# Where the tiles of a two-layer mixer lie in SBUF: a gap at its head, small constants at its end, one query and key buffer fewer

## The chip, the cores and the metric

The kernel runs on one core of a Trainium2 chip. The metric is the device time of one execution in microseconds (us). Operands are 32-bit throughout: the matrix products take them as float32r (4 bytes a column), and each product is made of three matrix multiplications, of high and low halves, to keep float32 accuracy.

## The reference

Two layers of a mixer with three parallel branches over 512 frames of 1024 channels. Cut to what matters:

```
for l in range(2):
    xn = rmsnorm(x, pre_g[l]);  proj = xn @ w_in[l]            # 1024 -> 7584 columns, split into u_a, v_a, z_a, ...
    y_a = u_a * (tril(w_s) @ layernorm(v_a) + b_s) * silu(z_a)       # blocks of 128 frames, 8 groups
    y_b = latent_attention(q_down, kv_down, k_rope) * silu(z_b)      # 8 heads, rotary part shared, chunk mask
    y_c = band_attention(q_c, k_c, v_c, rel_table) * silu(z_c)       # 8 heads, own chunk and 8 before, learned bias
    merged = sum_i sigmoid(g_i + gate_b_i) * (y_i @ w_branch[l, i])  # i over a, b, c; y_i is 512 wide
    x = x + rmsnorm(merged @ w_out[l], post_g[l])
```

## The kernel before

All products go through `mm3` (lines 112 to 115): three matmuls into one PSUM tile, high by high, high by low, low by high. The first operand of a matmul in the listing, `lhsT`, is the stationary one (128 columns, 512 bytes a partition, loaded by a weight load ahead of the matmul); the second, `rhs`, is the moving one, streamed column by column. The profile prints the moving one first: in `pm<-A_h,whi` the tile `A_h` moves and `whi` is stationary. Three kinds of product make up most of the work:

- `fm_unit` (line 197): weights `whi`, `wlo` are stationary, the normalised input `A_h`, `A_l` moves, 512 columns; 24 matmuls a unit.
- `tm_unit` (line 185): slices of `A_h`, `A_l` are stationary and weights move: 512 columns, or 416 in `mla_down`, or 256 twice for the very last unit (line 716).
- the branch products in `gate_units` (line 244 on): weights stationary, and `X` (branches a and c) or `ybh`, `ybl` (branch b) moving, 12 matmuls of 512 columns.

Each weight slice comes by a DMA from SP's queue into `wraw` (3 buffers), ScalarE copies it to `whi`, VectorE or GpSimd makes `wlo` from the rest (line 107; 4 buffers each).

The two attentions are spread over 64 steps a layer (line 655). A step issues the scores of one head and one block of 128 queries (256, 384 or 512 columns; lines 418 to 438), transposes the softmax of three steps earlier (line 361), and after each head makes the weighted sum (lines 378, 379). Between them the list `units` (line 643) is worked off by a credit in microseconds, with fixed rates (line 33): products fill TensorE while the other engines work on the softmax. The order of instructions is fixed when the program is built.

Query and key tiles come from `qtile` (line 142): one head of the latent attention holds four (`qa`, `ka`, `kl`, and the rotary stack `qr`, made by `rope_stack` from line 533), a pair of heads of the band attention six. `qr` of an odd head is made right after the other tiles of its pair.

Where a tile lies in SBUF follows from the listing alone. Pools are laid out one after the other in the order in which they are opened (lines 46 to 49: `cst`, `wp`, `wk`, `sm`), tiles in a pool in the order of their making, and every tile is rounded up to 32 bytes a partition. The first tile starts at byte 16512 of the partition. `ident` (512 bytes) and `mhalf` (32) stand first, so `A_h` starts at byte 17056 = 16 x 1024 + 672; `A_l`, `mrg`, `YT`, `X`, `vt` and `PT_h` follow at 672 past a multiple of 1024 as well, `PT_l` at 160. The constants of the two layers (`col_0`, `gbh_0`, `col_1`, `gbh_1`, 576 bytes) come next, and every tile of `wp` and `wk` then starts at 224 past a multiple of 1024, but `pp1` and `pp2` at 736. Slices that matmuls read start a multiple of 512 bytes into their tile, but the second half of a `mla_down` weight, 1664 bytes into it, and the slices of `X` at line 296, blocks of 256 bytes. So every operand of a float32r matmul starts 32 bytes past a multiple of 64. SBUF is full: the last tile ends 160 bytes before the end of the partition.

Of the kernel before, what the change touches and what calls it, by code (L numbers as in the profile page):

```python
# [8 lines left out]
F32 = mybir.dt.float32  # L9
F32R = mybir.dt.float32r  # L10
# [5 lines left out]
P = 128  # L16
L = 2
D = 1024
S = 512
KT = D // P  # L20
# [3 lines left out]
H = 8  # L24
# [16 lines left out]
def trunk_kernel(ctx, tc, x, wtm, wqd, wrv, wqk, wfm, wgate, wbr, wout,  # L41
                 cols, post_g, ln_g, ln_b, sgu_wt, rel, csnd, out):
    nc = tc.nc
    v_, s_, g_, t_ = nc.vector, nc.scalar, nc.gpsimd, nc.tensor

    cst = ctx.enter_context(tc.tile_pool(name="cst", bufs=1))
    wp = ctx.enter_context(tc.tile_pool(name="wp", bufs=4))
    wk = ctx.enter_context(tc.tile_pool(name="wk", bufs=1))
    sm = ctx.enter_context(tc.tile_pool(name="sm", bufs=4))
    psm = ctx.enter_context(tc.tile_pool(name="psm", bufs=3, space=PSUM))  # L50
    pss = ctx.enter_context(tc.tile_pool(name="pss", bufs=2, space=PSUM))
    pst = ctx.enter_context(tc.tile_pool(name="pst", bufs=2, space=PSUM))
    pso = ctx.enter_context(tc.tile_pool(name="pso", bufs=1, space=PSUM))
    dr = ctx.enter_context(tc.tile_pool(name="dr", bufs=1, space=bass.MemoryType.DRAM))

    ident = cst.tile([P, P], F32, name="ident")
    make_identity(nc, ident)
    mhalf = cst.tile([P, 1], F32, name="mhalf")
    g_.memset(mhalf, -0.5)

    A_h = cst.tile([P, KT, S], F32R, name="A_h")
    A_l = cst.tile([P, KT, S], F32R, name="A_l")
    mrg = cst.tile([P, KT, S], F32, name="mrg")
# [9 lines left out]
    PT_h = cst.tile([P, TB * PTS + P], F32R, name="PT_h")  # L73
    PT_l = cst.tile([P, TB * PTS + P], F32R, name="PT_l")
    x1 = dr.tile([S, D], F32, name="x1")


    ZB = 3 * PTS + 2 * P
# [61 lines left out]
        return mrg[:, 2 * tb:2 * tb + 2, :]  # L140

    def qtile(nm):
        return wk.tile([P, S], F32R, name=nm, tag="qk", bufs=12)

    def bk_t(n):
        return wk.tile([P, n], F32, name="bk", tag="bk", bufs=2)
# [28 lines left out]
        return i  # L175

    def load_consts(l):
        t = cst.tile([P, 4 * KT + H + 3], F32, name=f"col_{l}")
        nc.sync.dma_start(out=t, in_=cols[l])
        c = {"pre": t[:, 0:KT], "gb": t[:, KT:4 * KT], "sb": t[:, 4 * KT:4 * KT + H], "mg": t[:, 4 * KT + H:]}  # L180
        c["gbh"] = cst.tile([P, 3 * KT], F32, name=f"gbh_{l}")
        g_.tensor_scalar(out=c["gbh"], in0=c["gb"], scalar1=0.5, scalar2=None, op0=ALU.mult)
        return c

# [141 lines left out]
    def ca_qk(l, kind, p, qk):  # L326

        a, b = qtile("qa"), qtile("qb")
        kl = (qtile("kl"), qtile("kl")) if kind else None
        qk[(kind, p)] = (a, b, kl)  # L330
        lo, hi = slice(0, 64), slice(64, 128)

        def done(ps):
            if kind == 0:
                for t, r, o in ((a, lo, hi), (b, hi, lo)):
                    s_.activation(out=t[r], in_=ps[r], func=AF.Copy, scale=0.125)
                    v_.scalar_tensor_tensor(out=t[o], in0=ps[r], scalar=0.125, in1=f32(t[r]),
                                            op0=ALU.mult, op1=ALU.subtract)
            else:
                for t, u, r, o in ((a, kl[0], lo, hi), (b, kl[1], hi, lo)):  # L340
                    s_.copy(out=t[r], in_=ps[r])
                    v_.tensor_tensor(out=u[r], in0=ps[r], in1=f32(t[r]), op=ALU.subtract)
                    s_.copy(out=t[o], in_=ps[r])
                    g_.tensor_copy(out=u[o], in_=u[r])
        yield from fm_unit(wfm[l, kind * 4 + p], done)
# [187 lines left out]
    def rope_stack(h, d):  # L533

        r = qtile("qr")
        hh, j = divmod(h, 4)
        rs = slice(j * 32, j * 32 + 32)
        v_.tensor_copy(out=r[0:32], in_=YT[rs, 2 * hh, :])
        s_.copy(out=r[32:64], in_=YT[rs, 2 * hh + 1, :])
        g_.tensor_copy(out=r[64:128], in_=r[0:64])  # L540
        d[h] = r
# [44 lines left out]
    for tb in range(TB):  # L586
        for hf in range(2):
            nc.sync.dma_start(out=x_rows(tb)[:, hf, :], in_=x[tb * P:(tb + 1) * P, hf * 512:(hf + 1) * 512])
        if tb == 0:
            cl = [load_consts(0)]  # L590
            raws += [load_raw(wqd[0, j], 832) for j in range(2)]
        if tb == 1:
            raws.append(load_raw(wqd[0, 2], 832))
# [4 lines left out]
    for l in range(L):  # L598
        c = cl[l]
        qk, zc, zb, st = {}, {}, {}, {}  # L600
        ya, yc, yb = [], [], []
        if l == 0:
            dgen = mla_down(l, st, raws, first)
            del raws
            step(dgen)
            norm_x(2, c)
            norm_x(3, c)
            cl.append(load_consts(1))
        else:
            st = st1  # L610
# [44 lines left out]
        for i in range(NS + LAG + 1):  # L655
# [32 lines left out]
            while credit > 0 and units and units[0][0] <= i:  # L688
                t = next(units[0][1], None)
# [14 lines left out]
        for hf in range(2):  # L704
            t = bk_t(S)
# [117 lines left out]
```

## Time and profile before

| what | us |
|---|---|
| median of 3 runs (lowest, highest) | 1101.63 (1100.35, 1102.0) |
| the profiled execution's own time | 1102.16 |
| its span, first to last instruction | 1100.4 |
| TensorE busy in the span | 1075.0 |
| VectorE, ScalarE, GpSimd busy | 645.7, 529.2, 234.1 |

Times of the trace are counted from the start of the span. A matmul's printed duration (about 0.39 us for 512 columns) runs from the entry of its first column to the modelled end of its last result, and overlaps that of the next; the pace of TensorE is the distance from one matmul's start to the next one's. The views used here are the profile's page, the waits, the groups by line and shape, the windows (busy time by stretch) and the timeline (single instructions in order of time).

### The profile page before, as it was taken

What the parts mean: (1) busy time and instruction counts of PE and PEld (TensorE: products, weight loads), DVE (VectorE), ACT (ScalarE), POOL (GpSimd) and SP (SyncE); (2) the same over time, 40 slices, a digit from 0 to 9 for tenths busy, and PEclk for the clock granted to TensorE, in tenths of its full rate; (3) what the DMA queues carried; (4) which work ended last, traced back from release to release, by engine and by line L of the source; (5) the groups of instructions that cost most, each with busy time, mean ns of one, the idle gap of its engine ahead of it and who ended that gap; (6) DMA issues with size and microseconds to landing.
All of it is one profiled execution on the core that took longest, in us unless ns stands there. A gap on an engine that the chain in (4) does not pass through costs nothing.

```text
span 1100.4 us, 14199 instructions
## 1 busy us (share of the span) xinstructions
PE 1075.0 (98%) x5096; PEld 886.9 (81%) x5096; DVE 645.7 (59%) x1332; ACT 529.2 (48%) x1073; POOL 234.1 (21%) x249
## 2 busy tenths in 40 slices
PE   6999999999999999999999999999999999999997
PEld 4887878888888888888787787788888888888886
DVE  5674776666566654334577756675656665534443
ACT  6454576445454543224563644664544545432331
POOL 2310132221123231210033111331212323221000
PEclk9999999999999999999999999999999999999999
DMA  7231132223233223334342322212223232323342
GB/s 238 78 101 63 52 102 85 70 81 101 77 96 96 69 86 109 95 114 153 104 133 92 104 74 67 85 58 87 91 73 106 89 86 79 102 77 96 106 150 80
DMA packets 37703, 104.65 MB, mean 95 GB/s; under 512 B 5376, under 2 KB 6400, under 8 KB 37632
## 3 DMA queue, kind: packets, MB, share of 16 engines
q1 hardware_dynamic: 37632, 103.74, 30.3%
q8 instruction: 40, 0.66, 0.3%
q14 instruction: 31, 0.25, 0.1%
HBM read 99.53 MB, written 4.19 MB: 94 GB/s over the span
## 4 chain that ended last, share of the span: by engine, by line
PE 45%; ACT 2%; DVE 2%; issue 1%; POOL 1%; DMA 0%; POOLq 0%; DVEq 0%; ACTq 0%
PE pm L114 13%; PE pm L113 13%; PE pm L115 13%; PE pt L361 2%; PE po L379 1%; PE po L378 1%; DVE wlo L107 0%; PE ps_s L419 0%; PE ps_s L418 0%; PE ps_s L436 0%; PE ps_s L438 0%; PE ps_s L437 0%; POOL rs L136 0%; PE pt L167 0%; DMA wraw<-in_wtm_dram 0%
## 5 line engine op out<-in xcount | busy, mean ns | idle before, releaser
L102 ACT CAST whi<-wraw 128x1024 fp32r<-128x1024 f32 (+3 forms) x194 | 177.1, 914 | 263.2 <-PE pm L114 156.9
L113 PE MATMUL pm<-A_h,whi 128*128 128x512 f32 x640 | 259.9, 406 | 0.0
L114 PE MATMUL pm<-A_l,whi 128*128 128x512 f32 x640 | 252.8, 395 | 0.0
L115 PE MATMUL pm<-A_h,wlo 128*128 128x512 f32 x640 | 252.7, 395 | 0.0
L107 DVE TENSOR_TENSOR wlo<-wraw,whi 128x1024 fp32r<-128x1024 f32 (+3 forms) x130 | 152.0, 1172 | 113.2 <-ACT whi L102 109.7
L107 POOL TENSOR_TENSOR wlo<-wraw,whi 128x1024 fp32r<-128x1024 f32 (+1 forms) x64 | 116.2, 1815 | 379.7 <-ACT whi L102 311.7
L113 PE MATMUL pm<-whi,A_h 128*128 128x512 f32 (+2 forms) x456 | 177.9, 390 | 2.6 <-ACT A_h L172 2.6
L114 PE MATMUL pm<-wlo,A_h 128*128 128x512 f32 (+2 forms) x456 | 176.1, 387 | 1.1 <-DVE wlo L107 1.1
L115 PE MATMUL pm<-whi,A_l 128*128 128x512 f32 (+2 forms) x456 | 176.3, 387 | 0.4 <-DVE A_l L173 0.2
L115 PEld LDWEIGHTS pm<-A_h,wlo 128*128 128x128 f32 x640 | 120.1, 188 | 29.1
L114 PEld LDWEIGHTS pm<-A_l,whi 128*128 128x128 f32 x640 | 120.4, 188 | 25.2
L113 PEld LDWEIGHTS pm<-A_h,whi 128*128 128x128 f32 x640 | 120.2, 188 | 25.2
L113 PEld LDWEIGHTS pm<-whi,A_h 128*128 128x128 f32 x456 | 86.5, 190 | 20.2 <-ACT A_h L172 4.5
L115 PEld LDWEIGHTS pm<-whi,A_l 128*128 128x128 f32 x456 | 86.4, 189 | 17.4 <-DVE A_l L173 2.0
L114 PEld LDWEIGHTS pm<-wlo,A_h 128*128 128x128 f32 x456 | 86.5, 190 | 17.0 <-DVE wlo L107 2.2
L354 DVE TENSOR_SCALAR pp<-pp,st 128x128 f32<-128x128 f32 (+3 forms) x128 | 70.2, 549 | 3.6
L367 ACT CAST PT_h<-pt 128x128 fp32r<-128x128 f32 (+3 forms) x128 | 53.9, 423 | 32.1 <-PE pt L361 31.0
L423 DVE CUSTOM_DVE_ANT_0 pp<-ps_s,bk 128x128 f32<-128x128 f32 (+1 forms) x64 | 31.2, 487 | 60.4 <-PE ps_s L419 60.1
L368 DVE TENSOR_TENSOR PT_l<-pt,PT_h 128x128 fp32r<-128x128 f32 (+3 forms) x128 | 61.6, 481 | 6.5 <-ACT PT_h L367 6.1
L361 PE MATMUL pt<-ident,pp 128*128 128x128 f32 x320 | 55.9, 272 | 1.5 <-DVE X L212 1.5
L444 ACT ACTIVATE pp<-ps_s,st 128x128 f32<-128x128 f32 (+1 forms) x64 | 33.8, 528 | 43.4 <-DVE st L442 42.7
L426 ACT ACTIVATE pp<-pp,st 128x128 f32<-128x128 f32 (+1 forms) x64 | 36.0, 563 | 37.6 <-DVE st L425 36.9
(180 smaller groups left out, 1581.8 us busy)
## 6 DMA issues: line engine op xcount, KB each, us to landing
wraw<-in_wgate_dram SPq DMA_DIRECT2D x48, 512.0 KB, 3.6
wraw<-in_wtm_dram SPq DMA_DIRECT2D x32, 512.0 KB, 3.5
wraw<-in_wfm_dram SPq DMA_DIRECT2D x32, 512.0 KB, 3.6
wraw<-in_wbr_dram SPq DMA_DIRECT2D x48, 256.0 KB, 2.6
wraw<-in_wout_dram SPq DMA_DIRECT2D x16, 512.0 KB, 3.6
bk<-in_rel_dram SPq DMA_DIRECT2D x16, 256.0 KB, 2.7
wraw<-in_wqd_dram SPq DMA_DIRECT2D x8, 416.0 KB, 4.2
mrg<-in_x_dram SPq DMA_DIRECT2D x8, 256.0 KB, 6.9
```

The source lines that it names most:

```text
L102: s_.copy(out=hi[:, :cols], in_=raw[:, :cols])
L107: i = e.tensor_tensor(out=lo[:, :cols], in0=raw[:, :cols], in1=f32(hi[:, :cols]), op=ALU.subtract)
L113: t_.matmul(out=ps, lhsT=lh, rhs=rh, start=start, stop=False)
L114: t_.matmul(out=ps, lhsT=lh, rhs=rl, start=False, stop=False)
L115: t_.matmul(out=ps, lhsT=ll, rhs=rh, start=False, stop=stop)
L354: v_.tensor_scalar(out=pp[:, :n], in0=pp[:, :n], scalar1=rc, scalar2=None, op0=ALU.mult)
L361: t_.transpose(pt[:, kb * P:(kb + 1) * P], pp[:, kb * P:(kb + 1) * P], ident)
L367: s_.copy(out=dst(PT_h), in_=src)
L368: v_.tensor_tensor(out=dst(PT_l), in0=src, in1=f32(dst(PT_h)), op=ALU.subtract)
L423: v_.tensor_tensor_reduce(out=pp[:, :n], in0=ps[:, :n], in1=bias[:, S - n:S], scale=1.0, scalar=-3e38, op0=ALU.add, op1=ALU.max, accum_out=mx)
L426: s_.activation(out=pp[:, :n], in_=pp[:, :n], func=AF.Exp, bias=nm, accum_out=se)
L444: s_.activation(out=pp[:, :n], in_=ps[:, :n], func=AF.Exp, bias=nm, accum_out=se)
```

## The change

A tile `pad` of 480 float32 (1920 bytes) is placed first in `cst` and never used. `ident`, `mhalf` and the constants of the layers move to a new pool `cs` that is opened after `sm`. To make room, the query and key tiles have 11 buffers instead of 12. No instruction is added, taken out or changed, besides the places of its operands and what follows from the buffers.

By the rules above `A_h` then starts at 16512 + 1920 = 18432 = 18 x 1024; `A_l`, `mrg`, `YT`, `X`, `vt`, `PT_h` at multiples of 2048, `PT_l` at 512 past a multiple of 1024, `wraw`, `whi`, `wlo` and all of `wk` at multiples of 1024 (`pp1`, `pp2` 512 past one). Every operand of a float32r matmul but the two exceptions named starts at a multiple of 512, those at multiples of 128 and 256. `ident`, which moves in the transposes, stays at 128 past a multiple of 512.

```diff
+    cs = ctx.enter_context(tc.tile_pool(name="cs", bufs=1))
...
-    ident = cst.tile([P, P], F32, name="ident")
-    make_identity(nc, ident)
-    mhalf = cst.tile([P, 1], F32, name="mhalf")
-    g_.memset(mhalf, -0.5)
-
+
+    cst.tile([P, 480], F32, name="pad")
     A_h = cst.tile([P, KT, S], F32R, name="A_h")
...
     x1 = dr.tile([S, D], F32, name="x1")
+    ident = cs.tile([P, P], F32, name="ident")
+    make_identity(nc, ident)
+    mhalf = cs.tile([P, 1], F32, name="mhalf")
+    g_.memset(mhalf, -0.5)
...
     def qtile(nm):
-        return wk.tile([P, S], F32R, name=nm, tag="qk", bufs=12)
+        return wk.tile([P, S], F32R, name=nm, tag="qk", bufs=11)
...
-        t = cst.tile([P, 4 * KT + H + 3], F32, name=f"col_{l}")
+        t = cs.tile([P, 4 * KT + H + 3], F32, name=f"col_{l}")
...
-        c["gbh"] = cst.tile([P, 3 * KT], F32, name=f"gbh_{l}")
+        c["gbh"] = cs.tile([P, 3 * KT], F32, name=f"gbh_{l}")
```

## Rows read from the trace of the kernel before

**Rows 1.** The page: busy us (share) xinstructions, and TensorE's granted clock in 40 slices.
```profile
PE 1075.0 (98%) x5096; PEld 886.9 (81%) x5096; DVE 645.7 (59%) x1332; ACT 529.2 (48%) x1073; POOL 234.1 (21%) x249
PEclk9999999999999999999999999999999999999999
```

**Rows 2.** Waits of TensorE: us in total, times, longest us.
```profile
PE pt L167 <- DVE tmp L164: 10.2, 5, 7.1
PE pm L113 <- ACT A_h L172: 2.6, 2, 2.4
PE pt L361 <- DVE X L212: 1.5, 2, 0.8
```

**Rows 3.** Windows, columns as headed: attention in both layers, then gates alone.
```profile
core 0: us, PE busy (x) PEld busy (x) DVE busy (x) ACT busy (x) POOL busy (x), PEclk, DMA share, GB/s
150.00:250.00 100.00, 100.00 (x488) 83.44 (x487) 63.79 (x144) 55.02 (x116) 28.73 (x22) 1.00 0.28 85
1000.00:1050.00 50.00, 50.00 (x216) 40.06 (x215) 24.89 (x27) 17.88 (x25) 6.24 (x5) 1.00 0.41 120
```

**Rows 4.** Timeline of TensorE (start us, us, ...): gates of branch c, layer 2.
```profile
999.79 0.39 PE L113 MATMUL pm<-A_h,whi 128*128 128x512 f32 x1
...
1004.69 0.39 PE L113 MATMUL pm<-X,whi 128*128 128x512 f32 x1
```

**Rows 5.** The same view: output product of layer 1, then the end of layer 2's.
```profile
509.89 0.40 PE L113 MATMUL pm<-whi,A_h 128*128 128x512 f32 x1
...
514.79 0.40 PE L113 MATMUL pm<-whi,A_h 128*128 128x512 f32 x1
...
1084.68 0.39 PE L114 MATMUL pm<-wlo,A_h 128*128 128x512 f32 x1
...
1088.34 0.39 PE L115 MATMUL pm<-whi,A_l 128*128 128x512 f32 x1
```

**Rows 6.** The same view: a product of branch b.
```profile
411.17 0.39 PE L115 MATMUL pm<-ybh,wlo 128*128 128x512 f32 x1
...
412.53 0.39 PE L115 MATMUL pm<-ybh,wlo 128*128 128x512 f32 x1
```

**Rows 7.** The same view: the last unit, 256 columns a matmul.
```profile
1088.57 0.28 PE L113 MATMUL pm<-whi,A_h 128*128 128x256 f32 x1
...
1093.90 0.28 PE L115 MATMUL pm<-whi,A_l 128*128 128x256 f32 x1
```

**Rows 8.** The same view: scores of one block of queries, and the product after them.
```profile
102.85 0.28 PE L436 MATMUL ps_s<-ka,qa 128*128 128x256 f32 x1
...
103.21 0.39 PE L113 MATMUL pm<-whi,A_h 128*128 128x512 f32 x1
```

**Rows 9.** Groups of TensorE by line and shape: xcount | busy us, mean ns | idle before.
```profile
L113 PE MATMUL pm<-A_h,whi 128*128 128x512 f32 x640 | 259.9, 406 | 0.0
L113 PE MATMUL pm<-whi,A_h 128*128 128x512 f32 x376 | 149.2, 397 | 0.0
L361 PE MATMUL pt<-ident,pp 128*128 128x128 f32 x320 | 55.9, 272 | 1.5 <-DVE X L212 1.5
L113 PE MATMUL pm<-X,whi 128*128 128x512 f32 x128 | 51.2, 400 | 0.0
L113 PE MATMUL pm<-whi,A_h 128*128 128x416 f32 x64 | 24.3, 382 | 2.6 <-ACT A_h L172 2.6
L520 PE MATMUL pt<-ident,YT 128*32 128x128 f32 x8 | 1.5, 271 | 0.0
```

**Rows 10.** Timeline: rotary stack of head 3 on VectorE; last scores of head 1.
```profile
120.08 0.42 DVE L538 CAST qr<-YT 32x512 fp32r<-32x512 f32 x1
...
131.45 0.39 PE L438 MATMUL ps_s<-krs,qr 128*128 128x512 f32 x1
150.01 0.28 PE L438 MATMUL ps_s<-krs,qr 128*128 128x256 f32 x1
```

## The prediction

> **What bounds the kernel now.** I read the page first: TensorE is busy 98% of the span, and its granted clock is full in every slice, so the level is 2.4 GHz throughout [rows 1]. The waits come next: of the 25 us in which TensorE is idle, the largest wait is 10.2 us for `norm_x` at the joins of the stages, and inside the attention only single waits below a microsecond are left [rows 2]. The windows tell the same from the other side: in 100 us of attention TensorE is never idle while VectorE is busy 64%, and in the gate stage it is never idle at VectorE's 50% [rows 3]. No other engine and no transfer sets the pace over most of the span. The time is therefore the number of matmuls times the distance from one start to the next, and the question is what that distance depends on. Only the timeline shows it.
>
> At 2.4 GHz 512 columns enter in 213.3 ns and 256 in 106.7. The timeline shows more, and not the same everywhere:
> - Weights stationary, `A_h`/`A_l` or `X` moving: 4.90 us over 21 distances, 233.3 ns [rows 4].
> - `A` stationary, weights moving: 233.3 ns as well in the first half of the output product, yet 3.66 us over 16, 228.8 ns, in the second half [rows 5].
> - `ybh`/`ybl` moving: 1.36 us over 6, 226.7 ns [rows 6].
> - 256 columns, weights moving: 5.33 us over 47, 113.4 ns [rows 7]; 256 columns in the scores: 0.36 us over 3, 120 ns [rows 8].
>
> The first class is the same with the other engines at work and nearly idle, so they don't cause it. What differs is where the operands lie: `A` and `X` begin 672 past a multiple of 1024, weights, `yb` and the query tiles 224 past one. So the place in SBUF bears on the pace, by about 2% between classes, and all classes are 6 to 12% above bare entry.
>
> **How I read the distances.** Sixteen columns of 4 bytes, 64 bytes a partition, enter in 6.67 ns at 2.4 GHz. 113.4 ns is 17.0 of these, 226.7 is 34.0, 233.3 is 35.0, 120 is 18.0; 228.8 is 34.3, a mean. Bare entry would be 16 and 32. Every operand now starts 32 bytes past a multiple of 64 (the layout in the section on the kernel). If the moving operand is fetched in 64-byte pieces that start at multiples of 64, then 2048 bytes touch 33 pieces instead of 32 and 1024 bytes touch 17 instead of 16. No settled distance above is below 33 or 17, and the 256-column stream sits on 17 exactly. That is an estimate from five distances; no matmul of the trace with aligned operands at full rate contradicts or confirms it, since there is none (the transposes move an aligned `ident`, but at half this rate).
>
> **The change, part by part.** *The gap and the moved constants.* After it every moving and stationary operand starts at a multiple of 64, nearly all at multiples of 512. By the reading above each matmul loses one piece, 6.67 ns. How many are there? 5096 matmuls on the page [rows 1], less 464 transposes (six lines, the first and the last of them with x320 and x8 [rows 9]), makes 4632: 1920 with `A` moving (three lines of x640), 384 with `X`, 1128 with weights moving at 512 columns, 192 at 416 [rows 9], and the rest in branch b, the scores and the weighted sums.
> - 4632 x 6.67 ns = 30.9 us.
> - `sgu_mix` moves four blocks of 64 columns, so it loses four pieces each: 48 x 3 further pieces, 1.0 us more.
> - The `mla_down` matmuls of layer 1 are paced by loads and norms, as the waits on L167 and L113 [rows 2] show: 96 x 6.67 ns = 0.6 us not gained.
> - What is late next: a TensorE that is 3% faster reaches its waits earlier. The joins stay as long as they are. In attention VectorE at 64% [rows 3] has to do the same in 3% less time, which leaves it at 66%. Between nothing and one wait of 0.75 us (1.5 us, 2 times [rows 2]) for each of 32 heads, 24 us, I take 2 us, near the first end, since softmax is consumed three steps after it is made.
>
> Sum: 30.9 + 1.0 - 0.6 - 2.0 = 29.3 us less. The profiled execution took 1102.16 us (span 1100.4 and 1.8 around it), 0.5 above the median of the runs; 1102.2 - 29.3 = 1072.9, or 1072 on the median's footing.
>
> The bounds of the piece: I can't show that it vanishes. From below, the addresses might change nothing, or the distances might rise to the 120 ns that the scores take, one piece more [rows 8]. From above, everything beyond 33 and 16 pieces might go. One piece is the middle of these and what rows 7 have in excess.
>
> *Constants at the end.* `ident` keeps its place within 512 bytes and moves at half rate; `mhalf`, `col` and `gbh` are operands of single columns. Nothing on either side, hidden by a full TensorE [rows 3]. [...]
>
> *Eleven query and key buffers.* Twelve tiles are alive when `qr` of an odd head is made while the odd head of the pair before is still in use: `qr` of head 3 is cast at 120.08, head 1's last scores, which free four tiles, start at 131.45, and head 3 needs it at 150.01 [rows 10]. With eleven it has to be made after 131.7, still 18 us early. I count nothing, as a wait in that window meets a tile nobody yet needs. The far end: if the cast kept its place in VectorE's queue it would hold the splits and softmax behind it by 11.4 us, in three odd heads and one tile of the last pair in each layer, 8 x 11.4 = 91 us. I hold that for unlikely, as a buffer is only handed out behind its release and the cast can then be queued behind it.
>
> [...] The rows show that two places, both multiples of 32, differ by 2% [rows 4, 6]. If pieces are of 16 or 32 bytes, all operands already lie well, no piece is gained, and the classes differ for another reason; this is the third rival below. [...]
>
> [...]
>
> **The rivals.**
> 1. *All excess beyond one piece goes* (33 pieces at 512 columns, the classes become one): `A` and `X` moving and the slow 224 of the weights-moving matmuls lose 13.3 ns (2304 + 224: 33.7 us), 904 others 8.8 (8.0 us), the remaining 432 of 512 columns some 10 (4.3 us), 768 shorter ones one piece (5.1 us): 51 us less, 1051. For it: the classes' differences look like costs of place as well. Against it: rows 6 with 34.
> 2. *Only the relation of the two operands counts.* In rows 6 both lie at the same place modulo 512 and 34 pieces are the result; after the change all do. Then 2528 matmuls go from 35 to 34, and 904 from 34.3 to 34: 16.9 + 1.9 us less, 1083. Against it: the scores also have both at the same place and take 18, not 17.
> 3. *Address is not the cause*, or what it does is the same at 0 as at 32: 1102, within 0.2%.
> 4. *Slower: two reads that start at the same place collide.* Place: every product with `A`, where the operands now lie 64 bytes apart modulo 512. Price: rows 8 against rows 7, one piece: (1920 + 384 + 1128 + 192 + 48) x 6.67 ns = 24.5 us, 1126. It decides if rows like 4 come out above 233.3 ns. For it: 120 against 113.4 ns at 256 columns. Against it: rows 6, same place and the fastest of all with 512.
>
> **How the numbers follow.** One piece per matmul 0.45, with its own range 1057 (the 2304 of rows 4 lose a second piece, 15.4 us) to 1087 (half a piece in the mean). Rival 1: 0.17. Rival 2: 0.12. Rival 3: 0.11. Rival 4: 0.15, which takes in a loss through the buffers. 0.2% of the time, 2.2 us, is about what a measurement here can tell from none. Faster by more than that: 0.45 + 0.17 + 0.12 = 0.74; within it 0.11; slower 0.15. The range leaves out rival 4 and the low tail of rival 1: 1045 to 1103.
>
> **What would show it.** Right: rows 4's distance at 226.7 ns or less, rows 7's at 106.7 to 109, the stage of gates alone shorter by 3% with TensorE's clock unchanged, no new wait above a few us, `qr` of head 3 cast after 131 and before its head. Wrong: distances as now (rival 3), `A` moving at 226.7 with rows 7 unchanged (rival 2), distances above 233.3 or 113.4 (rival 4), or VectorE's casts at L538 waiting on TensorE with idle TensorE behind them (the buffers).

## The result and the profile after

The changed kernel takes 1084.65 us (median of 4 runs, 1083.68 to 1085.38) against 1101.0 us (1100.35 to 1102.0) before: ratio 0.985, interval 0.9833 to 0.9867. Its profiled execution took 1085.38 us with a span of 1083.7, so 16.7 us of span are gone. The forecast of 1072 us had the direction, and the time lies in its range; the likeliest case was not what happened. 1084.65 us is close to the 1083 us of the second rival, which had a chance of 0.12.

First the page of the changed kernel, to be read against [rows 1]: busy us (share), instructions, and the granted clock.

```profile
PE 1058.5 (98%) x5096; PEld 886.0 (82%) x5096; DVE 648.1 (60%) x1332; ACT 529.1 (49%) x1073; POOL 231.3 (21%) x249
PEclk9999999999999999999999999999999999999999
```

TensorE executes the same 5096 matmuls at the same granted clock (0.999 of full in the mean, 0.997 before), and is busy 16.5 us less. So it isn't waits that went. The waits of TensorE (us in total, times, longest us) say the same; all are those of [rows 2], two lines further down in the listing, within 0.2 us, and TensorE is idle 25.2 us of the span against 25.4:

```profile
PE pt L169 <- DVE tmp L166: 10.1, 5, 7.0
PE pm L115 <- ACT A_h L174: 2.8, 2, 2.6
PE pt L363 <- DVE X L214: 1.5, 2, 0.8
```

The windows answer to [rows 3], with the same columns: attention, then the gates alone (the second window begins 15 us earlier than before, as the stage does).

```profile
150.00:250.00 100.00, 100.00 (x495) 84.63 (x495) 65.71 (x147) 55.57 (x118) 27.81 (x23) 1.00 0.27 85
985.00:1035.00 50.00, 50.00 (x222) 41.38 (x222) 26.28 (x29) 18.76 (x26) 6.32 (x5) 1.00 0.42 129
```

TensorE is never idle in either, as before. In the same time it starts 222 matmuls of the gates instead of 216 and 495 of attention instead of 488, 2.8% and 1.4% more. VectorE rises to 66% in attention and still sets nothing.

The timeline of TensorE in the changed kernel (start us, us, ...) has the distances, in the order: scores of one block; transposes and what follows them, with a product of branch b; output product of layer 1; gates of layer 2; output product of layer 2 and the last unit.

```profile
103.30 0.28 PE L438 MATMUL ps_s<-ka,qa 128*128 128x256 f32 x1
...
103.66 0.40 PE L115 MATMUL pm<-whi,A_h 128*128 128x512 f32 x1
...
403.17 0.60 PE L363 MATMUL pt<-ident,pp 128*128 128x128 f32 x4
403.53 0.48 PE L115 MATMUL pm<-A_h,whi 128*128 128x512 f32 x1
403.84 0.40 PE L116 MATMUL pm<-A_l,whi 128*128 128x512 f32 x1
404.07 0.39 PE L117 MATMUL pm<-A_h,wlo 128*128 128x512 f32 x1
...
406.34 0.39 PE L115 MATMUL pm<-ybh,whi 128*128 128x512 f32 x1
...
407.48 0.39 PE L117 MATMUL pm<-ybh,wlo 128*128 128x512 f32 x1
...
503.14 0.39 PE L115 MATMUL pm<-whi,A_h 128*128 128x512 f32 x1
...
507.90 0.39 PE L115 MATMUL pm<-whi,A_h 128*128 128x512 f32 x1
...
984.83 0.39 PE L115 MATMUL pm<-A_h,whi 128*128 128x512 f32 x1
...
989.59 0.39 PE L115 MATMUL pm<-X,whi 128*128 128x512 f32 x1
...
1066.08 0.39 PE L115 MATMUL pm<-whi,A_h 128*128 128x512 f32 x1
...
1071.52 0.28 PE L115 MATMUL pm<-whi,A_h 128*128 128x256 f32 x1
...
1075.12 0.28 PE L115 MATMUL pm<-whi,A_h 128*128 128x256 f32 x1
```

What the reader is to see, distance by distance:
- `A` or `X` moving: 4.76 us over 21 distances, 226.7 ns, where [rows 4] have 233.3.
- Weights moving over `A`: 226.7 ns in layer 1 (503.14 to 507.90, 21 distances) and at the end of layer 2 (1066.08 to 1071.52, 24 distances in 5.44 us), where [rows 5] have 233.3 and 228.8.
- `yb`: 1.14 us over 5, 228 ns with rounding at both ends, against the 226.7 of [rows 6]: nothing gained.
- The last unit, 256 columns: 3.60 us over 30, **120.0 ns**, where [rows 7] have 113.4: longer. The scores stay at 120 ns (0.36 us over 3), as in [rows 8].
- Behind transposes the first distances are 0.31 and then 0.23 us, and it takes several matmuls until 226.7 is reached: averaged over the 84 places where `A` moves behind a group of transposes, the second distance is 231.5 ns, the fifth 228.1 and the eleventh 226.8.

Every class of 512 columns now settles at the distance of the fastest class before, and none settles below it. I took the mean distance of each class on both timelines, without the distances next to a transpose and those with a wait in them: `A` moving 233.36 to 227.81 ns (1828 distances, 10.2 us), `X` moving 233.28 to 227.18 (376, 2.3 us), weights moving at 512 columns 230.25 to 227.59 (1112, 3.0 us), `yb`, scores and weighted sums of 512 columns together 1.0 us, the last unit 0.3 us to the other side. That is 16.2 us of the 16.7 that the span lost; the scores and weighted sums of 256 and 384 columns give some 0.5 us more.

### The profile page after: what moved, and what is told of

Read it like the earlier page. It is cut to its first block, busy times and chain, and to the rows that moved or that the text cites. A ratio compares the mean times of both kernels' runs of the same rounds, so it can differ in the third digit from the quotient of the medians.

```text
span 1083.7 us, 14197 instructions
## 1 busy us (share of the span) xinstructions
PE 1058.5 (98%) x5096; PEld 886.0 (82%) x5096; DVE 648.1 (60%) x1332; ACT 529.1 (49%) x1073; POOL 231.3 (21%) x249
## 4 chain that ended last, share of the span: by engine, by line
PE 43%; ACT 3%; DVE 2%; issue 1%; DMA 1%; POOL 1%; POOLq 0%; DVEq 0%; ACTq 0%
PE pm L116 12%; PE pm L115 12%; PE pm L117 12%; PE pt L363 2%; PE po L381 1%; PE po L380 1%; ACT whi L104 0%; PE ps_s L421 0%; PE ps_s L420 0%; PE ps_s L438 0%; DMA wraw<-in_sgu_wt_dram 0%; PE ps_s L440 0%; DVE wlo L109 0%; PE ps_s L439 0%; ACT tmp L162 0%
## 5 line engine op out<-in xcount | busy, mean ns | idle before, releaser
L104 ACT CAST whi<-wraw 128x1024 fp32r<-128x1024 f32 (+3 forms) x194 | 177.4, 916 | 247.0 <-PE pm L116 146.7
L115 PE MATMUL pm<-A_h,whi 128*128 128x512 f32 x640 | 257.0, 402 | 0.0
L117 PE MATMUL pm<-A_h,wlo 128*128 128x512 f32 x640 | 249.8, 390 | 0.0
L116 PE MATMUL pm<-A_l,whi 128*128 128x512 f32 x640 | 249.5, 390 | 0.0
L115 PE MATMUL pm<-whi,A_h 128*128 128x512 f32 (+2 forms) x456 | 176.7, 388 | 2.8 <-ACT A_h L174 2.8
```

The source lines that it names most:

```text
L104: s_.copy(out=hi[:, :cols], in_=raw[:, :cols])
L115: t_.matmul(out=ps, lhsT=lh, rhs=rh, start=start, stop=False)
L116: t_.matmul(out=ps, lhsT=lh, rhs=rl, start=False, stop=False)
L117: t_.matmul(out=ps, lhsT=ll, rhs=rh, start=False, stop=stop)
```

## The experiments

**Which address counts? Two kernels that set the two readings against each other.** The first is the kernel before with 32 bytes ahead of everything: each operand starts at a multiple of 64, and all stay where they were relative to each other.

```diff
     cst = ctx.enter_context(tc.tile_pool(name="cst", bufs=1))
...
+    cst.tile([P, 8], F32, name="pad")
     ident = cst.tile([P, P], F32, name="ident")
```

> The kernel before with 32 bytes of gap at the head and nothing else: A, X at 704 and weights, yb, query tiles at 256 past a multiple of 1024, all operands at multiples of 64, their distance from one another as before (64 bytes modulo 512). Theory 'relation' (the pace depends on where moving and stationary operand start relative to one another): rows with A moving stay at 233.3 ns, time 1101 us within 0.3%. Theory 'piece' (each operand's own start modulo 64 counts): at least what the whole change gave, 1085 us or less, A moving at 227 ns or less.

Measured: 1100.66 us, ratio 0.9996 (0.9987 to 1.0006). The gates of layer 2 on its timeline:

```profile
1004.35 0.39 PE L114 MATMUL pm<-X,whi 128*128 128x512 f32 x1
...
1005.05 0.39 PE L114 MATMUL pm<-X,whi 128*128 128x512 f32 x1
```

Three distances in 0.70 us: still 233.3 ns, and over the whole timeline `A` moving has a mean of 233.35 ns, as before the change. The second is the other way round, the kernel after with its gap 32 bytes longer: every operand starts 32 past a multiple of 64, as before the change, and all keep one place relative to each other.

```diff
-    cst.tile([P, 480], F32, name="pad")
+    cst.tile([P, 488], F32, name="pad")
```

> The changed kernel with a gap 32 bytes longer: every operand 32 bytes past a multiple of 512, all still at the same place modulo 512. 'Relation': as the changed kernel, 1084.6 us within 0.3%, A moving at 226.7 ns. 'Piece': the gain goes, 1100 us or so, A moving at 233 ns.

Measured: 1084.03 us, ratio to before 0.9849 (0.9832 to 0.9865). The same stage:

```profile
1003.97 0.39 PE L115 MATMUL pm<-A_h,whi 128*128 128x512 f32 x1
...
1004.65 0.39 PE L115 MATMUL pm<-X,whi 128*128 128x512 f32 x1
```

0.68 us over three, 226.7 ns; the mean of `A` moving is 227.7 ns, against 227.8 after the change. Multiples of 64 without a common place give nothing; a common place without multiples of 64 gives all of it. The theory of the lost piece falls by both.

**Which part of the change?** The kernel after without the gap and with twelve buffers, so that only the constants are moved; the operands then start 128 past a multiple of 1024.

```diff
-    cst.tile([P, 480], F32, name="pad")
...
-        return wk.tile([P, S], F32R, name=nm, tag="qk", bufs=11)
+        return wk.tile([P, S], F32R, name=nm, tag="qk", bufs=12)
```

> Only the constants move behind the other pools; no gap, 12 buffers: operands at 128 past a multiple of 1024, all at the same place modulo 512. 'Relation' and 'piece' both: as the changed kernel, 1084.6 us within 0.3%, so that neither the gap nor the multiples of 1 KB nor the eleventh buffer matter. If multiples of 1 KB matter by themselves: between 1085 and 1101 us.

Measured: 1085.96 us, ratio 0.9869 (0.9854 to 0.9883), an interval that overlaps that of the whole change. Gates of layer 2:

```profile
984.78 0.39 PE L114 MATMUL pm<-A_h,whi 128*128 128x512 f32 x1
...
989.54 0.39 PE L114 MATMUL pm<-A_h,whi 128*128 128x512 f32 x1
```

4.76 us over 21, 226.7 ns: moving the small tiles away from between `A` and `X` and the rest is what counts, since it was the 576 bytes of the layers' constants that set the two groups apart (672 against 224 past a multiple of 1024). The gap and the loss of a buffer are not needed for that. All four runs (1085.86 us and more) lie above the four of the whole change (up to 1085.38); no run here tells what these 1.3 us between the medians are.

The buffers alone, in the kernel before:

```diff
-        return wk.tile([P, S], F32R, name=nm, tag="qk", bufs=12)
+        return wk.tile([P, S], F32R, name=nm, tag="qk", bufs=11)
```

> The kernel before with 11 query and key buffers and nothing else. If the buffer costs nothing, as I counted: 1101 us within 0.3%, and the cast of head 3's rotary stack after 131 us. If a wait on the freed buffer holds VectorE: slower, by up to 91 us, with TensorE idle in the attention.

Measured: 1100.65 us, ratio 1.0005 (0.9996 to 1.0014). On its timeline the rotary stack of head 3 is made 12 us later than in [rows 10], with a wait of 1.67 us on VectorE:

```profile
132.29 0.42 DVE L538 CAST qr<-YT 32x512 fp32r<-32x512 f32 x1 [1.67 <-PE ps_s L436]
```

and the waits of TensorE have nothing new; the longest is still that of `norm_x`:

```profile
PE pt L167 <- DVE tmp L164: 9.5, 5, 6.6
```

**Every place by itself.** This kernel leaves the mixer out and runs streams of 40 matmuls: the moving tile lies at a multiple of 512 bytes, the stationary one at 0, 32, ... 480 past one (`wa` to `wp`), with 512 columns, with 256, and with 512 in reverse order.

```diff
+    mv = cst.tile([P, 4, S], F32R, name="mv")
+    for i in range(16):
+        ws.append((cst.tile([P, S + 8], F32R, name="w" + "abcdefghijklmnop"[i]), 0))
...
+            t_.matmul(out=ps[:, :n], lhsT=w[:, e + (k % 4) * P:e + (k % 4 + 1) * P], rhs=mv[:, k % 4, :n],
+                      start=k == 0, stop=k == count - 1)
```

> A kernel that leaves the mixer out: it only runs streams of 40 matmuls, one moving tile at a multiple of 512, and nineteen stationary tiles that start 0, 32, 64, ... 480 bytes (wa to wp) and 4, 8 and 16 bytes (wq, wr, ws) past it; 512 columns, then 256, then 512 in reverse order. 'Relation': the settled distance depends on the stationary tile's place: wa 226.7 ns, wc (64 bytes, as A moving before the change) 233.3, wo (448, as weights moving before) 228.8 or 233.3; at 256 columns wa 120 and wo 113.3 ns. If another cause lies behind the classes (the three products' pattern, the other engines, PSUM), all nineteen give one distance. Unknown to every theory: whether a place is faster than wa; if one settles at 33 pieces, 220 ns, a layout with it would beat the changed kernel.

Its timeline (each row a stream; the next start less this start, over 40, is the mean distance). The letters shown: `wa` lies at 0, `wc` at 64, `wd` at 96, `wi` at 256, `wj` at 288, `wo` at 448.

```profile
24.98 9.50 PE L70 MATMUL pm<-mv,wc 128*128 128x512 f32 x40
34.32 9.52 PE L70 MATMUL pm<-mv,wd 128*128 128x512 f32 x40
...
80.80 9.24 PE L70 MATMUL pm<-mv,wi 128*128 128x512 f32 x40
89.88 9.49 PE L70 MATMUL pm<-mv,wj 128*128 128x512 f32 x40
...
136.52 9.33 PE L70 MATMUL pm<-mv,wo 128*128 128x512 f32 x40
...
182.87 4.96 PE L70 MATMUL pm<-mv,wa 128*128 128x256 f32 x40
...
192.40 4.72 PE L70 MATMUL pm<-mv,wc 128*128 128x256 f32 x40
196.96 4.96 PE L70 MATMUL pm<-mv,wd 128*128 128x256 f32 x40
...
309.81 9.50 PE L70 MATMUL pm<-mv,wo 128*128 128x512 f32 x40
```

No other engine works beside these streams, and at 512 columns they have the distances of the kernels. Settled means of the last 24 distances, by the place of the stationary operand less that of the moving one, against the kernels:

| place | streams, ns | kernels, ns |
|---|---|---|
| 0 | 226.7 | 226.7, `yb` before [rows 6] and all after |
| 64 | 233.3 | 233.3, `A` moving before [rows 4] |
| 192 and 448 | 228.9, and 448 once 233.3 | 228.8 and 233.3, weights moving before [rows 5] |
| 256 | 226.7 | |
| the others, steps of 32 | 232.1 to 234.4 | |
| 0, 256 columns | 120.0 | 120, scores [rows 8] and last unit after |
| 64 and 320, 256 columns | 113.3 and 117.8 | |
| 192 and 448, 256 columns | 117.8 | 113.4, last unit before [rows 7] |

So at 512 columns the relation repeats after 256 bytes, not after 512 as the rival had it, and at 256 columns the common place is among the slowest. The same place (448) settles at either of two distances, in rows of 9.33 us in one pass and 9.50 in the other, as the two halves of [rows 5] did. The last line of the table seems to differ, but the kernel with 11 buffers, whose operands of the last unit lie 448 from each other as in the kernel before, has the streams' number there: 5.53 us over 47, 117.7 ns.

```profile
1086.76 0.28 PE L113 MATMUL pm<-whi,A_h 128*128 128x256 f32 x1
...
1092.29 0.28 PE L115 MATMUL pm<-whi,A_l 128*128 128x256 f32 x1
```

In that kernel the second half of layer 2's output product, just ahead of it, stayed at 233.3 ns instead of going to 228.8. So this place has two settled distances at 256 columns too, and the 113.4 of [rows 7] is one of them.

**The relation moved on purpose.** Two kernels from the one after, with a tile between `A`, `X` and the rest: 256 bytes, which by the streams changes nothing, and 96, which by them should take all of the gain away, though every operand still starts at a multiple of 32.

```diff
+    cst.tile([P, 64], F32, name="pad2")
     x1 = dr.tile([S, D], F32, name="x1")
```

> The changed kernel with 256 bytes more between the first pool and the weights: A, X at multiples of 512, weights, yb and query tiles 256 past one. The streams by themselves gave 226.7 ns at 0 and at 256 alike. 'Relation modulo 256': as the changed kernel, 1084.6 us within 0.3%. If the whole 512 bytes (or equal places as such) mattered: near 1101.

Measured: 1083.89 us, ratio 0.9848 (0.9831 to 0.9864). Gates of layer 2, 18 distances in 4.08 us, 226.7 ns:

```profile
984.98 0.39 PE L116 MATMUL pm<-A_h,whi 128*128 128x512 f32 x1
...
989.06 0.39 PE L116 MATMUL pm<-X,whi 128*128 128x512 f32 x1
```

```diff
+    cst.tile([P, 24], F32, name="pad2")
     x1 = dr.tile([S, D], F32, name="x1")
```

> The same with 96 bytes: weights, yb and query tiles 96 past a multiple of 512, A and X at 0. From the streams: A or X moving at 234.3 ns (wd), weights moving at 233.3 (wf), yb at 226.7. 'Relation': slower than the kernel before, which has 229 ns in four fifths of the weights-moving matmuls: 2304 x 1 ns + 904 x 4 ns = 6 us, less 1 us in the attention, some 1106 us (ratio 1.004 to 1.006). 'Piece' (all operands are at multiples of 32): 1101 or less.

Measured: 1104.13 us, ratio 1.0034 (1.0021 to 1.0047): slower than before, though by a little less than the 1.004 to 1.006 expected. Output product of layer 1, 21 distances in 4.90 us, 233.3 ns; the mean of `A` moving is 234.0, near the 234.3 of the stream at 96:

```profile
508.20 0.39 PE L116 MATMUL pm<-whi,A_h 128*128 128x512 f32 x1
...
513.10 0.40 PE L116 MATMUL pm<-whi,A_h 128*128 128x512 f32 x1
```

Between two groups of tiles, 96 bytes instead of 256 cost 20.2 us here (1104.13 less 1083.89).

**Whose relation, and what of the load?** More streams without the mixer: the place changes with each matmul, so that either a matmul's own two operands agree (`own`) or it agrees with the weights loaded for the next one (`nxt`); the stationary tile has 64 or 32 columns instead of 128; and the place goes in steps of 4 bytes from 0 to 252.

```diff
+        mm(own, (wa, wb)[k % 2], 0, P, (mva, mvb)[k % 2], S, k, 48)
...
+        mm(nxt, (wb, wa)[k % 2], 0, P, (mva, mvb)[k % 2], S, k, 48)
...
+            stream(w, 0, mcols, mva, S, 48)
...
+        ps = stream(wa, e, P, mva, S, 36)
```

> Streams alone again, the mixer left out. First 40 as wa before: 226.7 ns. Then two streams in which moving and stationary tile both alternate between 0 and 64 past a multiple of 512: 'own', where each matmul's two operands agree and the stationary one loaded meanwhile for the next lies 64 off, and 'next', where the one loaded meanwhile agrees with the moving one and its own lies 64 off. If moving read and the weight load that runs beside it disturb each other: next 226.7 ns and own 229 to 234. If a matmul's own pair counts: the other way. Then stationary tiles of 64 and of 32 columns at 0 and 64: if the disturbance is the load's reading, the excess over 213.3 ns falls with the columns loaded; if the moving read alone makes it, it stays at 13 and 20 ns. Then the stationary tile at 0, 4, 8, ... 252 bytes: a map in steps of 4 bytes; a place under 226.7 ns would be one to build a layout on.

The rows of the narrow stationary tiles, at place 0 and 64 each (48 distances to the next start):

```profile
38.55 11.19 PE L65 MATMUL pm<-mva,wa 128*64 128x512 f32 x48
49.58 11.33 PE L65 MATMUL pm<-mva,wb 128*64 128x512 f32 x48
60.75 11.28 PE L65 MATMUL pm<-mva,wa 128*32 128x512 f32 x48
71.86 11.29 PE L65 MATMUL pm<-mva,wb 128*32 128x512 f32 x48
```

Settled, `own` and `nxt` both have 231.7 ns: neither pair alone gives 226.7, and that part decides nothing. With 64 columns loaded the two places have 230.0 and 232.7 ns, with 32 both have 231.7, where 128 columns gave 226.7 and 233.3: the difference of place shrinks with the load and is gone at 32, yet the pace doesn't come down to 226.7. Over the 213.3 ns that 512 columns take at 0.417 ns a column (bare entry, an estimate from 226.7 ns at 512 columns and 120.0 at 256 in the streams before and after these) that is an excess of 17 to 19 ns, so neither of the two outcomes expected came: it doesn't fall with the columns loaded, and it doesn't stay at 13 and 20. In steps of 4 bytes 226.7 is reached at 0, 120, 132, 144, 156, 204 and 252, most places lie between 230 and 235, the highest at 237.7 (164 bytes), and none settles below 226.7.

**Which data, which length?** The same streams with bfloat16, and with 448 down to 128 columns.

```diff
+    mh = cst.tile([P, 4, S], BF, name="mh")
+    wh = cst.tile([P, S + 256], BF, name="wh")
...
+    for n in (448, 384, 320, 256, 192, 128):
+        stream(wa, 0, mva, n, 40)
+        stream(wb, 0, mva, n, 40)
```

> Streams alone, the mixer left out: float32r 512 columns at the same place, then bfloat16 operands, 512 columns, the stationary tile 0, 32, 64, 128 and 192 bytes past the moving one's place, then float32r with 448, 384, 320, 256, 192 and 128 columns, each at 0 and at 64 bytes. If the disturbance belongs to reads of 4 bytes a column: bfloat16 gives one distance near 216 ns at all places, and float32r's excess grows with the columns (7 ns at 256, 13 at 512). If any moving read meets it: bfloat16 has classes too. At 256 columns 0 should give 120 and 64 give 113.3 ns, as before; whether the order turns over at 384 (175 and 170 ns in the kernels) decides whether 'same place is best' holds for wide matmuls alone.

The timeline: bfloat16 in one row of 200 and its last two, then 4-byte operands with 384, 320 and 256 columns at the common place (`wa`) and 64 away from it (`wb`); the last row starts the 192 columns.

```profile
17.03 43.34 PE L74 MATMUL pm<-mh,wh 128*128 128x512 bf16 x200
...
59.78 0.59 PE L74 MATMUL pm<-mh,wh 128*128 128x512 bf16 x2
...
76.40 7.12 PE L74 MATMUL pm<-mva,wa 128*128 128x384 f32 x40
83.36 7.22 PE L74 MATMUL pm<-mva,wb 128*128 128x384 f32 x40
90.43 6.02 PE L74 MATMUL pm<-mva,wa 128*128 128x320 f32 x40
96.29 6.03 PE L74 MATMUL pm<-mva,wb 128*128 128x320 f32 x40
102.15 4.96 PE L74 MATMUL pm<-mva,wa 128*128 128x256 f32 x40
106.95 4.88 PE L74 MATMUL pm<-mva,wb 128*128 128x256 f32 x40
111.66 4.61 PE L74 MATMUL pm<-mva,wa 128*128 128x192 f32 x40
```

In bfloat16 five places from 0 to 192 bytes have one distance, 215.9 ns (43.34 less 0.59 over 198): at these five, place plays no part. Two things differ there at once, since the profile's page of this run has a bfloat16 weight load at 98 ns in the mean and a 4-byte one at 195, so this run doesn't say which of them frees bfloat16. In 4 bytes at the common place the settled distance is 226.7, 173.3, 146.7 and 120.0 ns for 512, 384, 320 and 256 columns. From 256 to 512 that is 106.7 ns for 256 columns, 0.417 a column, the same from each of these lengths to the next; each lies 13.3 ns above its columns at this rate, an estimate carried on to no columns at all, and only 448 has 16.0 above. So, at these lengths, the 34 of [rows 6] and the 18 of [rows 8] are 32 + 2 and 16 + 2, one fixed price a matmul and not a share of its length.

64 bytes away from the common place the same streams have 202.2 ns at 448 columns (202.7 at the common place), 176.7 at 384 (173.3), 146.7 at 320 (146.7) and 117.8 at 256 (120.0). So the common place gains 3.4 ns at 384 columns, 6.6 at 512 (the earlier streams, 226.7 against 233.3) and next to nothing at 320 and 448. The 113.3 ns that the earlier streams had 64 away at 256 columns, and that was expected again, did not come back: there too, one place has settled at two distances.

## Why the prediction was right in sign and wrong in size

- **What bounds the kernel: right.** Time is the number of matmuls times their distance; the waits stayed and 16.2 of 16.7 us are in the distances. Where the prediction says 2.4 GHz, what is measured is 2.4 columns a ns: 226.7 ns [rows 6] less 120 [rows 8] is 106.7 for 256 columns; the page has the granted share alone, 0.997 of full in the mean. The transposes follow one another at 0.11 us for 128 columns (four in 0.60 us above, one in 0.27 [rows 9]), half of that rate.
- **That place in SBUF sets the classes: right**, and shown by streams with nothing else at work (226.7 ns at 0, 233.3 at 64). The prediction took this from rows in which VectorE was still busy about half of the time or more [rows 3].
- **"Each matmul loses one piece, 6.67 ns": wrong.** This is the step that failed, and with it the largest term of the sum. I read an excess common to all classes as a 64-byte piece begun early; the term was 30.9 us and what was there to have was 16.2. The kernel with all at multiples of 64 (1100.66 us) and the one with all 32 past them (1084.03 us) refute it in both directions. What stands in its place is the distance of the two operands from each other modulo 256 bytes. Before, `A` and `X` lay 448 past the weights, which makes 64 or 192 (stationary less moving place, modulo 256) by which of them moves; after, 0. That the kernel became faster all the same is luck as far as the piece goes: the change that put every operand on a multiple of 64 put the two operands at a common place as well.
- **The classes that were at the common place already had nothing to gain.** `yb`, scores and weighted sums were counted with 6.67 ns each and kept their distances but for some 1.5 us in all. The last unit, from which the piece was read as 113.4 - 106.7, became 6.6 ns slower a matmul. That unit was the row nearest to my reading, and it was another class, not a purer one; the kernel with 11 buffers shows that at the same places it can also run at 117.7 ns, which is no whole number of pieces.
- **`sgu_mix`, 1.0 us more, and `mla_down`, 0.6 less:** the first had the same ground as the piece and falls with it (from start to start, the 48 matmuls took 7.0 us before and 7.1 after); the second cannot be told from the waits around it.
- **New waits, 2.0 us: too much.** The waits at the joins and behind norms are those of before within 0.2 us.
- **Eleven buffers, nothing: right.** The cast of `qr` for head 3 on VectorE's timeline after:

```profile
131.76 0.42 DVE L540 CAST qr<-YT 32x512 fp32r<-32x512 f32 x1 [1.63 <-PE ps_s L438]
```

  It comes behind 131.7, as the lifetimes demanded, with 1.63 us of wait on VectorE and none on TensorE; the kernel with the buffers alone measures 1.0005. The far end of 91 us did not come near.
- **The second rival had the mechanism** and 1083 us. It had the period wrong (512 bytes instead of 256), and one of its signs failed: it wanted rows 7 unchanged, and they rose to 120.0 ns. Its objection, that the scores share a place and still take 18 pieces, was none: a common place costs two pieces, 13.3 ns, at every length tried from 256 to 512 columns but one. Its 18.8 us came to 15.5 (10.2 + 2.3 + 3.0), mostly because the matmuls behind transposes need some steps to settle: the mean of `A` moving is 227.8, not 226.7.
- **The fourth rival, two reads that collide at a common place,** is refuted at 512 columns by every kernel here. At 256 columns the last unit did go from 113.4 to 120.0 ns, which was its sign. With 47 such distances in the last unit that is 0.3 us.

One test that I had set for the likeliest case, gates shorter by 3%, was met (2.8%) by another mechanism: it didn't tell the two apart. The last unit did: it rose to 120.0 ns, where the piece wanted it at 106.7 to 109.

In this case the pace of one operand depends on where the other lies: streams with no other engine at work settle at 226.7 ns with both at a common place and at 234.3 with 96 bytes between them. In bfloat16 they take 215.9 ns at all five places tried.

**What stays open.** Why 256 bytes, and why 120 or 144 are as good as 0, no run tells. The streams with narrower loads make it likely that the weight load beside the matmul has a part in it, since the difference of place went with the columns loaded (6.6 ns at 128, 2.7 at 64, none at 32), but the two paired streams, meant to say which load, both gave 231.7 ns and did not. What makes one place settle at one of two distances is open too. No kernel tried here is faster than the changed one by more than the intervals.

## What to carry to other kernels

When all matmuls of one shape are a few per cent over what their columns alone take (0.417 ns a column here), and differ by operand, write down the address of both operands modulo 256 and sort the distances by the difference; for 4-byte matmuls of 512 columns put both at the same place (226.7 ns here, up to 237.7 at others), and keep odd-sized constants out of the space between them. For other widths measure first: here the common place gained half as much at 384 columns (3.4 ns against 6.6), nothing at 320 and 448, and lost 2.2 to 6.7 ns at 256. Before pricing a common excess as removable, look for a class that lacks it; here the fastest class on the timeline was also the floor. A test that two mechanisms both pass, like a stage shorter by 3%, should stand beside one that only one of them passes.

## What the runs showed of the hardware

- With 4-byte operands the distance of 512-column matmuls depends on the place of the stationary operand relative to the moving one, modulo 256 bytes (226.7 ns at 0 and at 256 alike): 226.7 ns at 0 and at six other places of the 64 in steps of 4 bytes, 228.3 to 237.7 at the rest. In bfloat16 it doesn't (215.9 ns at five places).
- At a common place a 4-byte matmul costs 13.3 ns over 0.417 ns a column at 256, 320, 384 and 512 columns; at 448 it costs 16.0, and at 192 and 128 columns streams run at 111.7 ns at both places tried.
- At 256 columns a common place is slower than 64 bytes apart (120.0 against 113.3 ns in one run and 117.8 in another).
- One place can settle at two distances: 448 bytes apart, 228.9 or 233.3 ns at 512 columns, in streams and in kernels, and 113.4 or 117.7 ns at 256 columns in kernels.
